# A fused decoder layer in fp32: latent attention's first queries in a stream of their own, stores on GpSimd's queue, first bias rows earlier

## The chip, the cores and the metric

The kernel runs on one core of a Trainium2 chip. The metric is device time in microseconds (us) of one execution; lower is better. Engines are named as in the profile: PE (TensorE matrix multiplies), DVE (VectorE), ACT (ScalarE), POOL (GpSimd), SP (SyncE, which here only issues DMAs).

## The reference

One decoder layer over 1024 tokens of width 1024, all in float32. Three mixers share one input projection and one output projection; then comes a mixture of experts. Only the mixers matter for this change:

```python
def hybrid_mixer(x, w_in, w_out, sink, bias_a, bias_b, q_norm_g, kv_norm_g, w_uq, w_ukv, cos, sin):
    h = x @ w_in
    h_a, h_b, h_c = jnp.split(h, [A_COLS, A_COLS + B_COLS], axis=-1)
    o_a = swa_sink_mixer(h_a, sink, bias_a)
    o_b = dilated_mixer(h_b, bias_b)
    o_c = mla_mixer(h_c, q_norm_g, kv_norm_g, w_uq, w_ukv, cos, sin)
    return jnp.concatenate([o_a, o_b, o_c], axis=-1) @ w_out

def mla_mixer(...):
    q = (rms_norm(c_q, q_norm_g) @ w_uq).reshape(Bsz, T, C_HEADS, C_NOPE + C_ROPE)
    kv = (rms_norm(c_kv, kv_norm_g) @ w_ukv).reshape(Bsz, T, C_HEADS, C_NOPE + C_V)
...
        s = jnp.where(key_pos[None, :] <= q_pos[:, None], s, NEG_INF)
        p = jax.nn.softmax(s, axis=-1)
        return jnp.einsum('bhqk,bkhd->bqhd', p.astype(v.dtype), v)
```

Mixer A is banded attention with a window of 128 (4 heads), mixer B three groups of dilated banded attention (4 heads each), each with a learned bias by distance. Mixer C is latent attention: 8 heads, dense and causal, with keys of 64 + 32 columns and values of 64. After them come a layer norm, the choice of an expert group and of 2 out of 32 experts a token, the experts, and a second layer norm.

## The kernel before

Every large product is made of three matmuls on split operands (`mm3`, lines 388 to 390: high x high, low x high, high x low), so each operand is first cut in a high part (ACT, line 376 or 380) and a low part (DVE, line 378 or 382).

The program is written as tasks. A task issues matmuls on PE and then steps on other engines; it names the tasks that it needs and the buffers that it takes and frees. `Order.run` (line 301) takes lists of tasks (streams) and writes all engines' instructions out in one order: at each turn it takes, among the heads of all streams, the task that can start first by its own cost table, and between those that tie, the stream that stands first in `STREAMS`. So the order on each engine is fixed when the program is built, and each engine works through its instructions in that order: one that waits holds up all that stand behind it on its engine.

The stages in order of time, from the profiled execution: input projections (to about 430 us, with mixers B and A between them from 137 us on), latent attention (about 445 to 615 us), output projection and choice of experts (to 724 us), 32 experts (to 1030 us), the last layer norm.

Of the projections of latent attention (`mla_units`), keys, values and queries are stored to DRAM in split form (`d_k`, `d_v`, `d_qr`, `d_qn`; function `out`, line 1299, 56 stores of 256 KB on SP's queue), and loaded again per head (`kqs`, lines 1431 to 1435) when latent attention begins; `vC` holds the values (line 1443).

The bias of mixer B's first group (g = 2 in `row_tasks`, line 476) is made so: POOL clears a small tile `ohr` and loads a one-hot table into it (lines 483, 484) and casts it to `oh` (486); PE multiplies it with the bias table (`psb`, 491); ACT copies out the rows (494); POOL stores them (`d_row`, 496), moves them skewed in DRAM (`d_shear`, 498) and loads the table `tb` (508). DVE needs `tb` to turn the first scores `S_B` into `P_B` (744).

In latent attention (`dense`, line 1459) scores `SC` go to PE, the masked maximum to DVE (1488), exponentials to ACT (1494), transposes `ptC` to PE (1517), the product with values `oC` to PE (834, 835). `fs_A` and `fs_C` (864) spread the normalizing factors `fb_A`, `fb_C`, which ACT writes (859), over the rows; `fs_A` belongs to the end of mixer A. Between these runs `part_tasks`: the part of the output projection that needs only mixers A and B's outputs. It loads them as `ofa` (POOL, 1608, four loads in all), cuts them to `oha`, multiplies (`ya`, 16 tasks of 12 matmuls), and adds the result to `xr` (DVE, 1636), which POOL stores (`d_zp`, 1637). The rest of the projection is `y`, from `oh`.

Of the kernel before, what the change touches and what calls it, by code (L numbers as in the profile page):

```python
# [51 lines left out]
WPOOL = ((0, 0), (0, 1))  # L52
OPOOL = ()
MMB = 6
STREAMS = 'VTGRLQNPlE'
LAT = 0.415
TIE = 0.06
EARLY = 2
# [284 lines left out]
class K:  # L343
# [534 lines left out]
    def phase_attention(self):  # L878
# [58 lines left out]
        def mixed(a, b):  # L937

            return [t for i, x in enumerate(a) for t in b[i * len(b) // len(a):(i + 1) * len(b) // len(a)] + [x]]

        for ui, u in enumerate(units):
            nm = u[2] if u[0] == "cols" else u[1]
            if u[0] == "mla":
                M[nm] = self.mla_units(ui, nm, lat)
                if nm == "q":
                    Pt += M["r"][:1] + mixed(M["k"] + M["v"], early["v"]) + mixed(M["r"][1:], early["q"][:4])
                    Pt += rowt[2][0] + mixed(M["q"], early["q"][4:])
            elif u[0] == "v":
                def begin(nm=nm):
                    vt[nm] = self.vp.tile([P, 8, 2, 4, HD], F32R, name="v" + nm, tag="v")  # L950
                    if nm == "B0":
                        vt["A"] = self.vp.tile([P, 8, 1, 4, HD], F32R, name="vA", tag="va")

                def dests(nm=nm):
                    d = [(0, 2, vt[nm])]
                    return d + [(256, 1, vt["A"]), (384, 0, kr)] if nm == "B0" else d

                if nm != "B0":
                    tk = self.v_tasks(ui, u, None, None, [])
                    last["v" + nm] = self.dilated_v(int(nm[1]), u[2], tk[1::2])  # L960
                    if nm == "B1":
                        early["v"] = list(tk)
                    else:
                        Pt += tk
                else:
                    tk = self.v_tasks(ui, u, begin, dests, ["v", "va"])
                    tk[0].deps = [last["vB2"]]
                    Pt += tk
                    last["v" + nm] = tk[-1]
                    krt = self.key_rope_tasks(kr, tk[-1])  # L970
                    Pt += krt
            elif nm[0] == "c":
                j = int(nm[1])

                pt_, lt_ = self.latent_unit(ui, u, "kv" if j == 2 else "q", 128 if j == 2 else 256, lat, j != 1,
                                            (2,) if j == 2 else (0, 1) if j == 1 else None)
                if ui == 0:
                    first2 = pt_
                elif ui == 1:
                    both = []  # L980
                    for i in range(4):
                        for t in (first2[2 * i:2 * i + 2] + pt_[2 * i:2 * i + 2]):
                            t.deps.append(there[2 * i + 1])
                            both.append(t)
                    Pt += both
                else:
                    Pt += pt_
                L += lt_
            else:
                cells[nm] = []  # L990
                bq[nm] = [Buf("qk"), Buf("qk")]
                tk = self.qk_tasks(ui, u, cells[nm], bq[nm])
                if ui == 7:
                    early["q"] = list(tk)
                    tk[0].deps = [lat["t", j] for j in range(3)]
                else:
                    Pt += tk
                last[nm] = tk[-1]
            for g in rows:
                if rows[g] == ui:  # L1000
                    Pt += rowt[g][1]
                if rows[g] == ui + 1 and g != 2:
                    Pt += rowt[g][0]
# [274 lines left out]
    def mla_units(self, u, which, lat):  # L1278
# [17 lines left out]

        def out(dst, t):
            for i in range(2):
                nc.sync.dma_start(dst(i), t[i].bitcast(F32))

        kw = dict(deps=deps, alloc=["mm", "ph"], free=["mm", "ph"])
        steps = [("A", 0.48), ("D", 0.6), ("A", 0.48), ("D", 0.6), ("T", 2.5)]
# [134 lines left out]
    def mla_tasks(self, deps, tr):  # L1437

        nc = self.nc
        self.sm = {}  # L1440

        def vload(b):
            nc.sync.dma_start(self.v[:, b].rearrange("p (g h) i d -> p g (h i d)", g=2).bitcast(F32), self.d_v[b])

        ld = [Task(lambda n=n: self.kq_load(n), 0, [[("T", 4.0)]], deps=deps + ([tr] if n % NSET else []),
                   alloc=["kq%d" % (n % NSET)] + (["v"] if n == 0 else [])) for n in range(8)]
        vt = [Task(lambda b=b: vload(b), 0, [[("T", 4.0)]], deps=[tr]) for b in range(8)]
        Q, TT, V = [], [], []
        for n in range(8):
            if n % 2 == 0:  # L1450
                cell = {}
            for qp in range(4):
                q, t, v = self.dense(n, qp, ld, vt, tr, cell)
                Q += q
                TT += t
                V += v
        return ld[:1] + vt[:2] + ld[1:2] + vt[2:4] + ld[2:3] + vt[4:] + ld[3:], Q, TT, V

    def dense(self, n, qp, ld, vt, tr, cell):

# [2 lines left out]
        nm = "C%d_%d" % (n, qp)  # L1463
        p, hd = divmod(n, 2)
        hf = qp // 2
        Q, TT, V = [], [], []
        Ps = {}

# [30 lines left out]
        for b in (2 * qp, 2 * qp + 1):  # L1499
# [3 lines left out]
            post = [("D", 0.08 + 0.00104 * w) for w in ws] + [("A", 0.2 + 0.00083 * w) for w in ws]  # L1503
            Q.append(Task(lambda b=b: qfn(b), sum(3 * max(0.109, w * 0.000417) for w in ws), post,
                          deps=[ld[n], tr], alloc=["mm"] * len(ws) + [pb[b]], free_at={i + 1: ["mm"] for i in range(len(ws))}))
        if qp == 3:
            Q[-1].free_pe = ["kq%d" % (n % NSET)]
        nk = 2 * qp + 2
        for j0 in range(0, nk, 2):
# [17 lines left out]
            first, last = qp % 2 == 0 and j0 == 0, qp % 2 == 1 and j0 == nk - 2  # L1527
            if first:
                cell["ob"] = Buf("o")
            if last and hd == 0 and hf == 0:  # L1530
                cell["otb"] = Buf("ot")

            def vfn(j0=j0, slots=slots, st=st, first=first, last=last):
                if first:
                    cell["o"] = self.buf("o", [P, 512], F32, name="o" + nm)
                o = cell["o"]
                for j in (j0, j0 + 1):
                    mine = [s for s, (jj, i) in enumerate(slots) if jj == j]
                    s0, w = mine[0] * P, len(mine) * P
                    c0 = (qp % 2) * 256 + slots[mine[0]][1] * P  # L1540
                    vh = self.v[:, j, n]
                    self.pv(o[:, c0:c0 + w], (vh.rearrange("p i d -> p (i d)"), vh[:, 0]),
                            [st[i][:, s0:s0 + w] for i in range(2)], first and j == j0)
                yield
                if last:
                    if hd == 0 and hf == 0:
                        cell["ot"] = self.buf("ot", [P, T], F32, name="o" + nm)
                    yield from self.unfold(cell["ot"][hd * HD:(hd + 1) * HD, hf * 512:(hf + 1) * 512], o, hd)

            V.append(Task(vfn, 0.43, [("A", 0.48), ("D", 0.6)] if last else [], deps=[tt, vt[j0 + 1]],  # L1550
                          alloc=([cell["ob"]] if first else []) + ([cell["otb"]] if last and hd == 0 and hf == 0 else []),
                          free=[cell["ob"]] if last else [], free_pe=["ph"]))
        if qp % 2 and hd:
            def factor():
                l = sm["l"][:, 4 * hf:4 * hf + 4, 2 * p:2 * p + 2, :]
                r = sm["rl"][:, 4 * hf:4 * hf + 4, 2 * p:2 * p + 2]
                nc.vector.tensor_tensor(r, l[:, :, :, 0], l[:, :, :, 1], ALU.add)
                nc.vector.reciprocal(r, r)

            def use(ps):  # L1560
                ot = cell["ot"][:, hf * 512:(hf + 1) * 512]
                nc.vector.tensor_tensor(ot, ot, ps, ALU.mult)
                nc.sync.dma_start(self.d_o[4 + p, :, hf * 512:(hf + 1) * 512], ot)

            ft = Task(factor, 0, [[("D", 0.2)]], deps=[Q[-1]])
            sp = self.spread_tasks(nm, lambda: sm["rl"][:, :, 2 * p:2 * p + 2], hf, use, [ft, V[-1]], [cell["otb"]] * hf)
            sp[0].deps = [ft]
            sp[1].deps = sp[1].deps + [V[-1]]
            V += [ft] + sp
# [440 lines left out]
    def phase_mixers(self):  # L2010

        self.wos = {}
        Pt, Q, TT, V, L, krt, vl = self.phase_attention()
        tr = Task(self.mla_open, 0, deps=[Pt[-1]] + L)
        ld, Q2, T2, V2 = self.mla_tasks(krt, tr)
        part, pl, wl, w1, xl, ya = self.part_tasks([tr, V[-1]])
        for n, b in YAQ:
            Q2[n].deps = Q2[n].deps + [ya[b, 1]]
        Y, R, G, E = self.out_tasks(Q2 + wl + w1, V2, w1, ya[7, 1])
        m = dict(E=E, V=[V + V2], R=R, T=[TT + T2], Q=[Q + Q2], L=[L], N=[vl], P=[Pt + [tr] + part + Y], l=[ld, pl, wl, xl], G=G)  # L2020
        self.ord.run([s for k in STREAMS for s in m[k]])


# [468 lines left out]
```

## Time and profile before

| | before |
|---|---|
| median of 3 runs | 1091.59 us (1088.22 to 1093.24) |
| profiled execution, its own time | 1088.41 us |
| its span, first to last instruction | 1086.7 us |
| mean granted clock of TensorE | 0.967 |
| PE busy | 1014.6 us, 93% of the span |
| DVE, ACT, POOL busy | 759.6, 689.7, 212.5 us |
| moved by DMA | 231.06 MB, mean 213 GB/s |

The sum of a change is made against the profiled execution, 1088.41 us; what lies around its span is 1.7 us. That execution is 3.2 us below the median of the three runs. A granted clock of 1 is 2.4 GHz, of 0.5 it is 1.2 GHz. Busy time of PE counts work at either clock.

### The profile page before, as it was taken

How to read it: one execution, taken by the hardware profiler on the slowest of the kernel's cores; microseconds unless marked ns; L12 is line 12 of the kernel's file. 1: busy time of each engine (PE TensorE's matmuls, PEld its weight loads, DVE VectorE, ACT ScalarE, POOL GpSimd, SP SyncE). 2: the span in 40 equal slices, each digit the busy share in tenths (PEclk: the TensorE clock that was granted, in tenths of full speed). 3: DMA queues.
4: the chain of work that ended last, by engine and by line, in shares of the span. 5: the costliest groups of instructions: out<-in, count | busy, mean ns of one | idle time of the engine just before them, and what ended most of it. 6: DMA issues, size and time to landing. Idle time of an engine off the chain costs nothing. (4 is left out here: it accounts for less than half of the span.)

```text
span 1086.7 us, 16593 instructions
## 1 busy us (share of the span) xinstructions
PE 1014.6 (93%) x5703; PEld 841.5 (77%) x5703; DVE 759.6 (70%) x1610; ACT 689.7 (63%) x1453; POOL 212.5 (20%) x235
## 2 busy tenths in 40 slices
PE   8998989999999998899999998969999999999971
PEld 7897878988798887788889777757777777777730
DVE  5465556345444657889687558789899999999747
ACT  5343456255443556889666435449999888898764
POOL 1011001501100203003100134422334222221123
PEclk9998989999999999999999999989999999999986
DMA  7177713422503234383662584649999999999283
GB/s 281 41 294 268 280 42 118 153 85 84 115 26 93 74 92 127 107 288 84 196 179 68 161 313 156 271 163 332 379 371 387 391 382 379 388 384 366 113 321 153
DMA packets 68631, 231.06 MB, mean 213 GB/s; under 512 B 13012, under 2 KB 18580, under 8 KB 54976
## 3 DMA queue, kind: packets, MB, share of 16 engines
q1 hardware_dynamic: 50064, 180.64, 47.1%
q0 software_dynamic: 17616, 46.18, 12.1%
q10 hardware_dynamic: 864, 3.15, 0.7%
q8 instruction: 46, 0.75, 0.3%
q14 instruction: 41, 0.34, 0.1%
HBM read 191.82 MB, written 58.02 MB: 230 GB/s over the span
## 5 line engine op out<-in xcount | busy, mean ns | idle before, releaser
L2192 DVE TENSOR_TENSOR el<-er,eh 128x1024 fp32r<-128x1024 f32 x188 | 226.1, 1221 | 22.4 <-ACT eh L2190 22.4
L2190 ACT CAST eh<-er 128x1024 fp32r<-128x1024 f32 x188 | 193.7, 1057 | 5.0 <-PE gu L390 3.1
L389 PE MATMUL gu<-el,xh 128*128 128x512 f32 x256 | 104.9, 410 | 0.0
L388 PE MATMUL gu<-eh,xh 128*128 128x512 f32 x256 | 103.8, 406 | 0.0
L390 PE MATMUL gu<-eh,xl 128*128 128x512 f32 x256 | 101.2, 395 | 1.0 <-DVE xl L378 1.0
L2025 POOL DMA_INDIRECT xg<-d_x,tok x32 | 43.7, 1367 | 159.4 <-PE gx L2208 138.0
L1494 ACT ACTIVATE PC<-PC,mnC 128x512 f32<-128x512 f32 (+3 forms) x96 | 58.6, 616 | 20.0 <-DVE mnC L1488 19.8
L389 PEld LDWEIGHTS gu<-el,xh 128*128 128x128 f32 x256 | 48.2, 188 | 21.7 <-DVE el L2192 12.9
L388 PE MATMUL psv_B<-wh,xH 128*128 128x256 f32 (+1 forms) x192 | 60.4, 315 | 1.7 <-ACT wh L376 1.7
L389 PE MATMUL psv_B<-wl,xH 128*128 128x256 f32 (+1 forms) x192 | 59.5, 310 | 0.2 <-DVE wl L378 0.2
L748 ACT ACTIVATE P_B<-P_B,negm_B 128x128 f32<-128x128 f32 (+1 forms) x96 | 42.4, 443 | 26.4 <-DVE negm_B L744 26.4
L390 PE MATMUL psv_B<-wh,xL 128*128 128x256 f32 (+1 forms) x192 | 59.1, 308 | 0.0
L2030 POOL DMA_INDIRECT d_y<-y,idx x32 | 40.3, 1259 | 90.5 <-ACT y L2247 84.1
L390 PEld LDWEIGHTS gu<-eh,xl 128*128 128x128 f32 x256 | 48.1, 188 | 10.7 <-DVE xl L378 1.4
L388 PEld LDWEIGHTS gu<-eh,xh 128*128 128x128 f32 x256 | 48.1, 188 | 10.1
L388 PE MATMUL y<-eh,hh 128*128 128x512 f32 x128 | 52.8, 412 | 0.7 <-ACT hh L376 0.7
L378 DVE TENSOR_TENSOR plC<-ptC,phC 128x512 fp32r<-128x512 f32 (+1 forms) x80 | 46.7, 630 | 7.0 <-ACT phC L376 6.6
L389 PE MATMUL y<-el,hh 128*128 128x512 f32 x128 | 50.6, 395 | 0.0
L390 PE MATMUL y<-eh,hl 128*128 128x512 f32 x128 | 50.4, 393 | 0.0
L376 ACT CAST phC<-ptC 128x512 fp32r<-128x512 f32 (+1 forms) x80 | 38.7, 548 | 8.5 <-PE ptC L1517 8.2
L378 DVE TENSOR_TENSOR xl<-gx,xh 128x512 fp32r<-128x512 f32 x64 | 43.5, 684 | 0.0
L2247 ACT COPY y<-y 128x512 f32<-128x512 f32 x64 | 37.6, 588 | 8.3 <-PE y L390 4.4
(452 smaller groups left out, 2903.6 us busy)
## 6 DMA issues: line engine op xcount, KB each, us to landing
er<-in_w_gu SPq DMA_DIRECT2D x63, 1024.0 KB, 16.5
er<-in_w_dn SPq DMA_DIRECT2D x32, 1024.0 KB, 15.2
wr<-in_w_qk SPq DMA_DIRECT2D x36, 256.0 KB, 3.9
fy<-d_y SPq DMA_DIRECT2D x7, 1024.0 KB, 11.8
d_vb<-vs_B POOLq DMA_DIRECT2D x16, 256.0 KB, 2.7
kqs<-d_k SPq DMA_DIRECT2D x16, 256.0 KB, 4.8
kqs<-d_qn SPq DMA_DIRECT2D x16, 256.0 KB, 4.8
vC<-d_v SPq DMA_DIRECT2D x8, 512.0 KB, 6.3
```

The lines of the kernel that those rows point to most:

```text
L376: nc.scalar.copy(h, src)
L378: (low or nc.vector).tensor_tensor(l, src, h.bitcast(F32), ALU.subtract)
L388: nc.tensor.matmul(out, st[0], mv[0], start=start, stop=False, **kw)
L389: nc.tensor.matmul(out, st[0], mv[1], start=False, stop=False, **kw)
L390: nc.tensor.matmul(out, st[1], mv[0], start=False, stop=stop, **kw)
L748: nc.scalar.activation(p[:, i, :w], p[:, i, :w], AF.Exp, bias=negm()[:, b, hh:hh + 1], scale=-1.0, accum_out=l()[:, b, hh:hh + 1])
L1494: nc.scalar.activation(pt[:, c:c + w], pt[:, c:c + w], AF.Exp, bias=mn[:, 1:2], scale=-1.0, accum_out=sm["l"][:, b, n, i:i + 1])
L2025: self.nc.gpsimd.indirect_dma_start(out=xg, out_offset=None, in_=self.d_x1, in_offset=bass.IndirectOffsetOnAxis(ap=tok.bitcast(U32), axis= ...
L2030: return self.nc.gpsimd.indirect_dma_start(out=self.d_y, out_offset=bass.IndirectOffsetOnAxis(ap=idx.bitcast(U32), axis=0), in_=y, in_offs ...
L2190: nc.scalar.copy(hi[:, s], t[:, s])
L2192: nc.vector.tensor_tensor(lo[:, s], t[:, s], hi[:, s].bitcast(F32), ALU.subtract)
L2247: nc.scalar.copy(y[e][:, s], ps)
```

## The change

Three things are changed.

1. The first two score tasks of latent attention (head 0) leave the queries' stream and form a stream `q` of their own, one place later in priority. For the first two heads the query pairs are taken in the order 2, 3, 0, 1, and not 0, 1, 2, 3; the buffers of the keys and of the output are taken and freed to suit. Six of the eight loads of values are put ahead of the second head's keys.
2. `out` in `mla_units` issues its 56 stores from POOL and no longer from SP.
3. The matmuls of the first bias rows (`rowt[2][1]`) stand after the sixth task of the latent queries, and no longer at the end of their unit.

```diff
-STREAMS = 'VTGRLQNPlE'
+STREAMS = 'VTGRLQqNPlE'
...
-                    Pt += rowt[2][0] + mixed(M["q"], early["q"][4:])
+                    mq = mixed(M["q"], early["q"][4:])
+                    Pt += rowt[2][0] + mq[:6] + rowt[2][1] + mq[6:]
...
-                if rows[g] == ui:
+                if rows[g] == ui and g != 2:
                     Pt += rowt[g][1]
...
         def out(dst, t):
             for i in range(2):
-                nc.sync.dma_start(dst(i), t[i].bitcast(F32))
+                nc.gpsimd.dma_start(dst(i), t[i].bitcast(F32))
...
-            for qp in range(4):
+            for qp in ((2, 3, 0, 1) if n < 2 else range(4)):
...
-        return ld[:1] + vt[:2] + ld[1:2] + vt[2:4] + ld[2:3] + vt[4:] + ld[3:], Q, TT, V
+        return ld[:1] + vt[:6] + ld[1:2] + vt[6:] + ld[2:], Q, TT, V
...
+        order = (1, 0) if p == 0 else (0, 1)
...
-        if qp == 3:
+        if qp % 2 and hf == order[1]:
             Q[-1].free_pe = ["kq%d" % (n % NSET)]
...
-        m = dict(E=E, V=[V + V2], R=R, T=[TT + T2], Q=[Q + Q2], L=[L], ...
+        m = dict(E=E, V=[V + V2], R=R, T=[TT + T2], Q=[Q + Q2[2:]], q=[Q2[:2]], L=[L], ...
```

Each engine issues the same instructions as before, in another order; only the 56 stores change queue. From the first `y` matmul on, PE's order is the same as before. Three places show what moved (a row is a line of the program, an operation, and output and inputs with their sizes; a line after the edits has one or two added).

**POOL, the first bias rows.** The difference, with `qr` and `q` the rotary and plain latent queries on their way to DRAM:

```order
+L1300 DMA d_qr_77<-qr11h_1094 128x512
+L1300 DMA d_qr_77<-qr11l_1095 128x512
 L483 MEMSET ohr2_1103 33x384
 L484 DMA ohr2_1103<-in_c_onehot 33x383
 L486 CAST oh2_1106<-ohr2_1103 33x384
-L496 DMA d_row_82<-rows2_1260 4x383
-L498 DMA d_shear_83<-d_row_82 128x1532
-L508 DMA tb2_1335<-d_shear_83 128x4x256
+L1300 DMA d_qn_76<-q0_0h_1108 128x512
+L1300 DMA d_qn_76<-q0_0l_1109 128x512
+L1300 DMA d_qn_76<-q0_1h_1124 128x512
+L1300 DMA d_qn_76<-q0_1l_1125 128x512
```

Before, clearing and loading `ohr` followed the loads of `vB`; now eight stores of rotary queries stand ahead of them, of which the last two are shown. Behind the cast of `oh` stand eight stores of plain queries (four shown), then `d_row`. On PE the two `psb` matmuls stand 36 matmuls of 512 columns sooner than before: right behind the fourth tile of plain queries, and no longer behind the eighth.

**PE, the end of mixer A.** `S_A` are the last scores of mixer A's second pair but for one block, `fs_A` and `pt_A` its factors and transposes. Before:

```order
L390 MATMUL S_A_4_1_4507<-h_kA,l_qA_4126 128x256
L864 MATMUL fs_A_0_4600<-ident,fb_A_0_4573 128x128 x4
L777 MATMUL pt_A_0_0_4611<-ident,P_A_0_0_4504 128x128 x2
L777 MATMUL pt_A_0_1_4616<-ident,P_A_0_1_4525 128x128 x2
L864 MATMUL fs_A_1_4623<-ident,fb_A_1_4609 128x128 x4
```

Now, up to the second `fs_A`:

```order
L390 MATMUL S_A_4_1_4507<-h_kA,l_qA_4126 128x256
L388 MATMUL SC_2_4_0_4603<-kqs_4311 128x512
L389 MATMUL SC_2_4_0_4603<-kqs_4311 128x512
L390 MATMUL SC_2_4_0_4603<-kqs_4311 128x512
L388 MATMUL SC_2_4_512_4607<-kqs_4311 128x128
L389 MATMUL SC_2_4_512_4607<-kqs_4311 128x128
L390 MATMUL SC_2_4_512_4607<-kqs_4311 128x128
L864 MATMUL fs_A_0_4617<-ident,fb_A_0_4573 128x128 x4
L777 MATMUL pt_A_0_0_4627<-ident,P_A_0_0_4504 128x128 x2
L864 MATMUL fs_A_1_4636<-ident,fb_A_1_4625 128x128 x4
```

Six score matmuls of latent attention's query block 4 come between, and six more of block 5 follow behind the next transposes. The first `ya` has about as much PE work ahead of it as before.

**POOL and PE, the end of latent attention.** POOL before, where `d_zp` stores a finished tile of `ya` and `ofa` is the load for the last four `ya`:

```order
L1637 DMA d_zp<-xr_1_6762 128x512
L1637 DMA d_zp<-xr_0_6764 128x512
L1608 DMA ofa_6919<-d_o 128x4x256
L1637 DMA d_zp<-xr_1_6766 128x512
L1637 DMA d_zp<-xr_0_6921 128x512
L1637 DMA d_zp<-xr_0_6964 128x512
```

POOL now:

```order
L1639 DMA d_zp<-xr_1_6579 128x512
L1610 DMA ofa_6826<-d_o 128x4x256
L1639 DMA d_zp<-xr_0_6581 128x512
L1639 DMA d_zp<-xr_1_6828 128x512
L1639 DMA d_zp<-xr_0_6830 128x512
L1610 DMA ofa_6965<-d_o 128x4x256
L1639 DMA d_zp<-xr_1_6832 128x512
```

And PE now, where the last load's `ya` begin:

```order
L390 MATMUL ya_1_6950<-woh_1_5309,oha_6869 128x512
L388 MATMUL ya_1_6950<-woh_1_5311,oha_6869 128x512
L389 MATMUL ya_1_6950<-wol_1_5312,oha_6869 128x512
L390 MATMUL ya_1_6950<-woh_1_5311,oha_6869 128x512
L388 MATMUL ya_0_6983<-woh_0_5297,oha_6975 128x512
L389 MATMUL ya_0_6983<-wol_0_5298,oha_6975 128x512
```

The last `ofa` stands behind the eleventh of sixteen `d_zp`, before and now. Before, PE had fifteen transposes, the twelfth `ya`, the last sixteen `oC` and `fs_C` between the eleventh `ya` and the first that needs this load; now only the twelfth `ya` lies between. Eight `ya` follow the last `oC` on PE, where it was four, and two of the eight come ahead of the last `fs_C`, which before followed that `oC` at once. On ACT and DVE the order of all of latent attention is new as well.

## Rows read from the trace of the kernel before

**Rows 1.** Page, part 1: busy time of each engine, share of the span, instructions.

```profile
PE 1014.6 (93%) x5703; PEld 841.5 (77%) x5703; DVE 759.6 (70%) x1610; ACT 689.7 (63%) x1453; POOL 212.5 (20%) x235
```

**Rows 2.** Timelines of ScalarE and PE, 87 to 89 us: start, us, row, idle before and releaser.

```profile
87.94 1.15 ACT L376 CAST wh<-wr 128x512 fp32r<-128x512 f32 x2
...
88.62 0.50 PE L388 MATMUL ps_qB<-xH,wh 128*128 128x512 f32 x1 [2.20 <-ACT wh L376]
```

**Rows 3.** Answer on one tensor: the values' stores, shortest, median and longest in ns.

```profile
L671 POOL DMA_DIRECT2D d_vb<-vs_B x16: 539/540/565, 55.8 to 209.1; - x16
```

**Rows 4.** Timeline of GpSimd, the first bias rows and the next one-hot load.

```profile
93.60 0.44 POOL L483 MEMSET ohr<- 33x384 f32 x1
94.33 0.58 POOL L484 DMA_DIRECT2D ohr<-in_c_onehot  x1 [0.29 <-POOL ohr L483]
112.70 0.49 POOL L486 CAST oh<-ohr 33x384 fp32r<-33x384 f32 x1 [17.79 <-DVE qr11l L378]
125.17 0.53 POOL L496 DMA_DIRECT2D d_row<-rows  x1 [11.97 <-ACT rows L494]
...
135.20 0.80 POOL L508 DMA_DIRECT2D tb<-d_shear  x1 [4.67 <-DMA d_shear<-d_row]
...
136.72 0.55 POOL L484 DMA_DIRECT2D ohr<-in_c_onehot  x1 [0.29 <-POOL ohr L483]
140.72 0.50 POOL L486 CAST oh<-ohr 33x384 fp32r<-33x384 f32 x1 [3.44 <-DMA ohr<-in_c_onehot]
```

**Rows 5.** Timeline of VectorE, the two rows that end GpSimd's and PE's waits.

```profile
111.88 0.69 DVE L378 TENSOR_TENSOR qr11l<-t,qr11h 128x512 fp32r<-128x512 f32 x1 [0.73 <-ACT qr11h L376]
...
140.56 0.29 DVE L744 CUSTOM_DVE_ANT_0 P_B<-S_B,tb 128x128 f32<-128x128 f32 x1 [6.19 <-DMA tb<-d_shear]
```

**Rows 6.** Timeline of PE around the bias rows and the first scores.

```profile
111.81 0.40 PE L388 MATMUL mpq<-ch,wh 128*128 128x512 f32 x1
...
120.24 0.33 PE L491 MATMUL psb<-oh,relbh 33*4 33x384 f32 x1
...
141.26 0.59 PE L388 MATMUL S_B<-h_kB,h_qB 64*128 64x128 f32 x2 [3.08 <-DVE negm_B L744]
```

**Rows 7.** Waits of GpSimd, whole span, for the one-hot table's load.

```profile
POOL oh L486 <- DMA ohr<-in_c_onehot: 12.6, 3, 5.8
```

**Rows 8.** By stretch: length, busy PE, PEld, DVE, ACT, POOL (x rows), clock, DMA share, GB/s.

```profile
141.20:147.20 6.00, 5.94 (x24) 5.23 (x25) 3.92 (x22) 4.82 (x21) 0.01 (x1) 0.50 0.00 0
429.70:460.60 30.90, 25.44 (x185) 21.22 (x185) 25.02 (x81) 24.25 (x76) 0.55 (x1) 0.94 0.42 121
460.60:518.80 58.20, 56.35 (x415) 51.47 (x414) 51.11 (x140) 53.11 (x144) 11.41 (x10) 1.00 0.63 187
518.80:612.50 93.70, 93.24 (x602) 83.52 (x601) 67.88 (x165) 56.56 (x147) 8.72 (x15) 1.00 0.48 142
614.60:618.30 3.70, 3.70 (x12) 3.05 (x13) 1.50 (x3) 0.45 (x1) 0.00 (x0) 0.54 0.25 91
```

**Rows 9.** Timeline of PE, the wait at the start of latent attention.

```profile
435.02 0.66 PE L864 MATMUL fs_A<-ident,fb_A 128*128 128x128 f32 x4 [2.94 <-ACT fb_A L859]
```

**Rows 10.** Timelines of PE, VectorE, GpSimd and ScalarE, 606 to 630 us.

```profile
614.59 0.93 PE L864 MATMUL fs_C<-ident,fb_C 128*128 128x128 f32 x4 [1.83 <-ACT fb_C L859]
...
629.13 0.50 PE L388 MATMUL y<-woh,oh 128*128 128x512 f32 x1 [1.18 <-ACT oh L1719]
...
606.63 0.69 DVE L1636 SCALAR_TENSOR_TENSOR xr<-xr,ya 128x512 f32<-128x512 f32 x1 [2.11 <-PE ya L390]
...
607.61 0.54 POOL L1637 DMA_DIRECT2D d_zp<-xr  x1 [2.25 <-DVE xr L1636]
608.15 0.76 POOL L1608 DMA_DIRECT2D ofa<-d_o  x1
...
613.40 0.62 ACT L376 CAST oha<-ofa 128x512 fp32r<-128x512 f32 x1
```

**Rows 11.** Answer on one tensor: landing of the load of mixer A's outputs.

```profile
DMA to landing us min/median/max: 7.4/7.4/7.4
```

More of the change, by code (lines that the diff above doesn't have):

```diff
@@ L1529, in dense @@
                 cell["ob"] = Buf("o")
-            if last and hd == 0 and hf == 0:
+            if last and hd == 0 and hf == order[0]:
                 cell["otb"] = Buf("ot")
@@ L1545, in vfn @@
                 if last:
-                    if hd == 0 and hf == 0:
+                    if hd == 0 and hf == order[0]:
                         cell["ot"] = self.buf("ot", [P, T], F32, name="o" + nm)
@@ L1550, in dense @@
             V.append(Task(vfn, 0.43, [("A", 0.48), ("D", 0.6)] if last else [], deps=[tt, vt[j0 + 1]],
-                          alloc=([cell["ob"]] if first else []) + ([cell["otb"]] if last and hd == 0 and hf == 0 else []),
+                          alloc=([cell["ob"]] if first else []) + ([cell["otb"]] if last and hd == 0 and hf == order[0] else []),
                           free=[cell["ob"]] if last else [], free_pe=["ph"]))
@@ L1565, in dense @@
             ft = Task(factor, 0, [[("D", 0.2)]], deps=[Q[-1]])
-            sp = self.spread_tasks(nm, lambda: sm["rl"][:, :, 2 * p:2 * p + 2], hf, use, [ft, V[-1]], [cell["otb"]] * hf)
+            sp = self.spread_tasks(nm, lambda: sm["rl"][:, :, 2 * p:2 * p + 2], hf, use, [ft, V[-1]], [cell["otb"]] * (hf == order[1]))
             sp[0].deps = [ft]
@@ L2019, in phase_mixers @@
         Y, R, G, E = self.out_tasks(Q2 + wl + w1, V2, w1, ya[7, 1])
-        m = dict(E=E, V=[V + V2], R=R, T=[TT + T2], Q=[Q + Q2], L=[L], N=[vl], P=[Pt + [tr] + part + Y], l=[ld, pl, wl, xl], G=G)
+        m = dict(E=E, V=[V + V2], R=R, T=[TT + T2], Q=[Q + Q2[2:]], q=[Q2[:2]], L=[L], N=[vl], P=[Pt + [tr] + part + Y], l=[ld, pl, wl, xl], G=G)
         self.ord.run([s for k in STREAMS for s in m[k]])
```

## Prediction

> **What bounds the kernel now.** I read the busy times first: PE works 93% of the span and no other engine over 70% [rows 1]. PE takes its instructions in a fixed order, so a change in order is worth what PE idles, and what TensorE's clock loses after PE has idled; a busy stretch can give nothing. The stretches [rows 8] show where idle time is left in latent attention: 5.5 us of 30.9 at its start, 1.9 us of the next 58.2, 0.5 us of the last 93.7. The start also has a granted clock of 0.94, which loses 0.06 x 30.9 = 1.9 us. All that a better order could win there is 5.5 + 1.9 + 0.5 + 1.9 = 9.8 us. Then I read the timelines where the change puts hands on: PE's wait ahead of the first scores of mixer B, 3.08 us [rows 6], which ends when VectorE has `tb` [rows 5]; PE's wait for `fb_A`, 2.94 us [rows 9]; and those at the end of latent attention, 1.83 and 1.18 us [rows 10]. After the first of these the clock stood at 0.50 for 6.0 us, after the third at 0.54 for 3.7 us [rows 8]: lost 3.0 and 1.7 us. So a wait of PE costs itself and up to 3 us more.
>
> **Stores on GpSimd's queue.** SP loses 56 issues. Would its weight loads, which stood behind them, free PE? PE's one long wait among the latent units, 2.20 us, ends with a cast on ScalarE that starts with no idle time ahead of it [rows 2]: ScalarE was busy, not short of data, and its order there is unchanged. So 0; were a late weight load behind it after all, the bound is a gain of 2.2 + 3.0 = 5.2 us. On GpSimd a store of this size takes 0.54 us to issue [rows 3]. The 40 stores of keys, values and `vs_B` between 55.8 and 93.6 us take 40 x 0.54 = 21.6 us of 37.8, so GpSimd keeps up. The stored tensors are next read when latent attention loads its heads, some 300 us later; that covers any later landing.
>
> Those 16 samples also weigh a rule. The Trainium skill (SBUF — State Buffer, the section on two separate sides, and the one on the bandwidth-pool intuition) says that a DMA issued from GpSimd waits while VectorE holds the port that both share, and gives 620 ns alone and 3100 ns beside a VectorE copy. By it the 40 stores would take an estimated 124 us and GpSimd would run some 86 us late. The longest of the 16 is 565 ns beside a working VectorE; the trace does not agree, and this stands below as a rival of small weight.
>
> **First bias rows.** `psb` moves 36 matmuls forward: from 120.24 to 111.81 us [rows 6], 8.4 us. But the one-hot table that it needs is late. Before, its load was issued at 94.33 us [rows 4], long ahead. Now GpSimd, in order, first has the store of `qr11l` in its queue, which waits for VectorE to end at 111.88 + 0.69 = 112.57 [rows 5]. Then come 0.54 for that store, 0.44 to clear, 0.29 + 0.55 to issue the load, the landing, and 0.50 for the cast [rows 4]. Landing is the unknown: 3.44 us in the next case [rows 4], 5.8 at most over three [rows 7]. `oh` is there at 118.3 to 120.7, about when it was used before, and PE, which stands at `psb` from 111.8, waits 6.5 to 8.9 us. I take the middle, 7.7. What the clock loses afterwards is bounded by 1.7 and 3.0; I take 3.0, from the wait nearest in length. Queued behind that load are sixteen stores of plain queries, `d_row`, `d_shear` and `tb`. Eight stores come before `d_row`: 120.7 + 4.3 = 125.0, as early as before (125.17), and from there to VectorE's use of `tb` took 15.4 us [rows 4, 5]; with the other eight stores' 4.3 that ends by 144.7. PE reaches the scores 6.5 to 8.9 us later than the 138 it stood there, so by 144.7 to 147. The old wait of 3.08 and its 3.0 of clock are gone. Sum: 7.7 + 3.0 - 6.1 = **+4.6 us** (bounds 6.5 + 1.7 - 6.1 = +2.1 and 8.9 + 3.0 - 6.1 = +5.8). The wait for rows has moved from `tb` to `oh` and grown.
>
> **Latent attention's first scores.** Six score matmuls now stand ahead of the first `fs_A`, and more behind it, in PE's wait of 2.94 us [rows 9]; if that wait goes, the half clock of this stretch (1.9) goes too: **-4.8 us**. What is late next is ScalarE: busy 24.25 of these 30.9 us [rows 8], it gets the exponentials of those scores earlier, among the last ones of mixer A and ahead of the second pair's factors. So the gain may be nothing, or the wait may come back there (+2.9); at best all idle time and clock of the three stretches goes (-9.8). I take the two named items, half of that. The values' loads now ahead of the second head's keys cost nothing: head 0 alone is a stage of many microseconds, and four loads at about half a microsecond of issue each stand in front.
>
> **End of latent attention.** Two `ya` (24 matmuls, 5.6 us at 8.43 / 36 = 0.234 each) now fill the wait of 1.83 us for `fb_C`, and the 1.18 us ahead of `y` have four more `ya` in front: gone are 1.83 + 1.7 + 1.18 = 4.7 us. But the last `ofa` is now due one `ya` after the store that stands ahead of it on GpSimd. From the end of that `ya`: 0.98 to the store's issue, 0.54 for it, 0.76 for the load's issue, landing, 0.62 for the cast. Before, it had landed by 613.40, 4.5 us after its issue or sooner [rows 10]; the other bounds are 3.44 for the one-hot load and 7.4 us from issue to landing for the one `ofa` that was seen [rows 11]. PE has one `ya` in hand, 2.8 us. Wait: 0.98 + 0.54 + 0.76 + 4.5 + 0.62 - 2.8 = 4.6 us, and the clock's 1.7 of this place: 6.3 - 4.7 = **+1.6 us** (3.5 + 1.7 - 4.7 = +0.5 to 6.7 + 3.0 - 4.7 = +5.0). From `y` on nothing moves; all later work starts as much later or sooner.
>
> **Sum.** 0 + 4.6 - 4.8 + 1.6 = +1.4 us on the profiled 1088.41, so 1089.8 for that execution. It lies 3.2 us below the median of the three runs; on the median of 1091.59 the forecast is **1093.0 us**. About 0.5%, 5.5 us, is what a measurement of this kernel can tell from no change: no visible change.
>
> **Rivals.**
> - *ScalarE sets the pace* (slower, 0.25). At the end of mixer A and in the first two heads ScalarE and VectorE are busy 24 to 25 of 30.9 us and 51 to 53 of 58.2 [rows 8], so scores put early only push mixer A's exponentials and `fb_A` back. It decides from the point at which the new exponentials ahead of the second `fb_A` take longer than the new score matmuls on PE. Then the start gives 0 to +2.9: +6.2 to +9.1, about 1099. Against it: PE's wait falls where VectorE and ScalarE have gaps too.
> - *GpSimd's new waits do not bite* (faster, 0.12): `qr11l` and the loads come early enough that `psb` and the last `ya` wait under 1 us each. Then -5.1 - 4.8 - 3.7 = -13.6, 1078. This is what the change says it does. Against it stands GpSimd's order.
> - *The new order keeps PE full* (faster, 0.15): all 9.8 us are won and GpSimd's waits are at their short ends: +2.1 - 9.8 + 0.5 = -7.2, 1084.4.
> - *GpSimd falls behind its stores* (slower, 0.03): each issue stretches several times over, as it did in none of the 16; the queue's delay goes one to one into `psb`, and to fall behind at all takes 37.8 / 40 = 0.95 us an issue. At 1.3 us it would be 40 x 1.3 - 37.8 = 14 us late: about 1107 or above. The Trainium skill's page on SBUF is the ground for it.
>
> **How the numbers follow.** The forecast has 0.45; its own bounds, with the start of latent attention held, are 1091.59 + 2.1 - 4.8 + 0.5 = 1089.4 and 1091.59 + 5.8 - 4.8 + 5.0 = 1097.6. For 8 in 10 the range takes in the slower rival to 1101 and the second faster one, down to 1083; left out are the first faster rival, the last one and the far edges. Chances: faster 0.12 + 0.15 = 0.27, same 0.45, slower 0.25 + 0.03 = 0.28.
>
> **What would show it.** In the new profile: a wait of PE at `psb` of 6.5 to 8.9 us that ends on GpSimd's cast of `oh`, a half clock behind it, and no wait for `tb`. No wait of 2.9 us at the first `fs_A`, and a clock of about 1 from 430 to 461 us of the old time. At the end no wait at the last `fs_C`, but one of 3.5 to 6.7 us at the `ya` that needs the last `ofa`. From the first `y` on, the same length as before. The prediction is wrong if PE does not wait at `psb`, if the second `fs_A` waits as long as the first did, or if GpSimd's issues last more than 0.6 us.

## The result and the profile after

| | before | after |
|---|---|---|
| median of 6 runs each, one chip | 1089.76 us (1087.74 to 1093.24) | 1098.61 us (1095.14 to 1101.45) |
| ratio, 95% interval | | 1.0066 [1.0037, 1.0095] |
| span of the profiled execution | 1086.7 us | 1097.4 us |
| mean granted clock | 0.967 | 0.967 |

By the ratio the change costs 7.2 us [4.0, 10.4]; the medians of six lie 8.9 us apart. The forecast was +1.4 us, "no visible change"; the measured time lies within its range, but beyond the 0.5%, near the rival that was priced at about 1099. One run further on, of `after_prep_ofa`, took 2067.27 us for a cause that is not known and is left out of its ratio.

Page, part 1, of the kernel after, against [rows 1]:

```profile
PE 1014.6 (92%) x5703; PEld 839.7 (77%) x5703; DVE 758.8 (69%) x1610; ACT 690.0 (63%) x1453; POOL 240.9 (22%) x291
```

PE does the same work in the same busy time; the loss is idle time. POOL has 56 instructions and 28.4 us more. Waits of PE after (releaser, us in total, times, longest), those that the prediction spoke of or that changed:

```profile
PE psb L491 <- POOL oh L486: 5.6, 1, 5.6
...
PE ya L388 <- ACT oha L376: 5.1, 1, 5.1
PE ps_c L388 <- ACT xH L366: 3.5, 1, 3.5
PE ps_qB L388 <- ACT wh L376: 3.4, 1, 3.4
...
PE ptC L1519 <- ACT PC L1496: 1.6, 1, 1.6
...
PE SC L388 <- DVE negm_A L744: 1.3, 1, 1.3
PE y L388 <- ACT oh L1721: 1.2, 1, 1.2
...
PE fs_A L864 <- ACT fb_A L859: 0.4, 1, 0.4
```

The wait ahead of the first `S_B` [rows 6] is gone, that for `fb_A` has fallen from 2.94 [rows 9] to 0.4, that at the last `fs_C` (1.83) is gone, as a row below shows, and that ahead of `y` [rows 10] stands as it was. New are `psb`, `ya`, `SC` for `negm_A` and `ptC` for `PC`. (A wait at `psv_B` for `wh` is 1.7 us before, 2.7 here and 0.8 in the second profile of after: chance.) GpSimd's timeline after shows what `psb` and `ya` waited for:

```profile
114.26 0.54 POOL L1300 DMA_DIRECT2D d_qr<-qr11h  x1 [2.21 <-ACT qr11h L376]
114.99 0.54 POOL L1300 DMA_DIRECT2D d_qr<-qr11l  x1 [0.19 <-issue]
115.52 0.44 POOL L483 MEMSET ohr<- 33x384 f32 x1
116.25 0.56 POOL L484 DMA_DIRECT2D ohr<-in_c_onehot  x1 [0.29 <-POOL ohr L483]
119.19 0.50 POOL L486 CAST oh<-ohr 33x384 fp32r<-33x384 f32 x1 [2.39 <-DMA ohr<-in_c_onehot]
...
123.97 0.52 POOL L496 DMA_DIRECT2D d_row<-rows  x1
...
135.65 0.78 POOL L508 DMA_DIRECT2D tb<-d_shear  x1 [3.09 <-DMA d_shear<-d_row]
...
617.39 0.54 POOL L1639 DMA_DIRECT2D d_zp<-xr  x1 [2.68 <-DVE xr L1638]
617.92 0.76 POOL L1610 DMA_DIRECT2D ofa<-d_o  x1
```

The table's clearing stands behind the store of `qr11l`, and the cast 2.39 us behind its issue. `d_row` went out at 123.97, 1.2 us sooner than before, and `tb` at 135.65, 0.4 us later [rows 4]; counted from this trace's late start, 2.8 us by 49 us (table below), that is 4.0 and 2.4 us sooner. PE has no wait for `tb` left, but one of 5.6 us at `psb`. PE's timeline at the new waits, at the end of mixer A, and at three of the `fs_C`:

```profile
119.74 0.48 PE L491 MATMUL psb<-oh,relbh 33*4 33x384 f32 x1 [5.64 <-POOL oh L486]
...
436.18 0.50 PE L388 MATMUL SC<-kqs 96*128 96x512 f32 x1 [1.31 <-DVE negm_A L744]
440.19 1.11 PE L864 MATMUL fs_A<-ident,fb_A 128*128 128x128 f32 x4 [0.42 <-ACT fb_A L859]
...
486.37 0.66 PE L864 MATMUL fs_C<-ident,fb_C 128*128 128x128 f32 x4 [0.67 <-ACT fb_C L859]
...
515.31 0.63 PE L864 MATMUL fs_C<-ident,fb_C 128*128 128x128 f32 x4 [0.91 <-DVE plC L378]
...
603.25 1.75 PE L1519 MATMUL ptC<-ident,PC 128*128 128x128 f32 x14 [1.60 <-ACT PC L1496]
...
612.99 0.60 PE L864 MATMUL fs_C<-ident,fb_C 128*128 128x128 f32 x4
...
624.24 0.79 PE L388 MATMUL ya<-woh,oha 128*128 128x512 f32 x1 [5.07 <-ACT oha L376]
```

And the stretches (columns as in [rows 8]): around `psb`, behind `SC`, behind the last `fs_C`, around `ya`, then latent attention in three parts.

```profile
116.00:123.00 7.00, 3.26 (x8) 2.13 (x9) 2.39 (x4) 1.54 (x3) 4.34 (x9) 0.53 0.65 234
436.30:444.00 7.70, 7.13 (x27) 5.57 (x28) 7.28 (x31) 7.56 (x28) 0.56 (x1) 0.57 1.04 227
612.90:616.60 3.70, 3.70 (x20) 3.04 (x18) 1.48 (x3) 0.00 (x0) 0.54 (x1) 1.00 0.43 156
620.90:628.20 7.30, 3.96 (x9) 3.09 (x10) 1.29 (x2) 1.14 (x2) 0.00 (x0) 0.55 0.60 206
432.80:463.70 30.90, 27.73 (x191) 23.13 (x188) 26.91 (x85) 26.54 (x82) 0.56 (x1) 0.89 0.71 209
463.70:521.40 57.70, 54.30 (x406) 49.83 (x405) 48.74 (x133) 51.48 (x138) 12.22 (x11) 1.00 0.64 175
521.40:607.60 86.20, 84.30 (x557) 75.08 (x556) 63.52 (x162) 55.54 (x147) 5.11 (x9) 1.00 0.38 110
```

After the waits at `psb`, `SC` (1.3 us only) and `ya`, PE worked at half clock for 3 to 7 us; behind the last `fs_C` the clock stands at 1. In latent attention PE is idle for 3.2 + 3.4 + 1.9 = 8.5 us where it was 5.5 + 1.9 + 0.5 = 7.9 [rows 8]: the start has less, the two later parts more; 0.67, 0.91 and 1.60 us of it are the waits at 486, 515 and 603 us. And the start's clock fell from 0.94 to 0.89.

To place the loss I matched PE's instructions of two traces by name and compared their starts. Each figure is what a kernel lost in that segment (us) against the first profile of before:

| profile | to 49 us | to the first `S_A` (407) | to the first `y` (629) | to the last expert (1021) |
|---|---|---|---|---|
| before, second profile | +2.1 | -2.7 | +0.3 | +0.8 |
| after | +2.8 | 0.0 | +6.9 | +0.4 |
| after, second profile | +1.9 | -1.1 | +7.1 | +0.4 |

The first segment is the same code in all of them and differs by chance: its wait `ps_c` was 3.5 us in one profile and 1.8 in another. The second spreads by 2.7 between two executions of before. The loss that stands out is that between `S_A` and `y`: the end of mixer A and latent attention. What the second segment costs has to come from the runs.

### The profile page after: what moved, and what is told of

Read it like the earlier page. It is cut to its first block, busy times and chain, and to the rows that moved or that the text cites. A ratio compares the mean times of both kernels' runs of the same rounds, so it can differ in the third digit from the quotient of the medians.

```text
span 1097.4 us, 16609 instructions
## 1 busy us (share of the span) xinstructions
PE 1014.6 (92%) x5703; PEld 839.7 (77%) x5703; DVE 758.8 (69%) x1610; ACT 690.0 (63%) x1453; POOL 240.9 (22%) x291
## 4 chain that ended last, share of the span: by engine, by line
PE 72%; DVE 9%; issue 7%; DMA 6%; ACT 5%; POOL 1%; SPq 0%; DVEq 0%; POOLq 0%; ACTq 0%
PE gu L389 6%; PE gu L390 5%; PE gu L388 5%; PE y L388 4%; PE y L390 4%; PE y L389 4%; PE psv_B L388 2%; PE psv_B L389 2%; PE psv_B L390 2%; PE ps_qB L390 2%; PE ps_qB L388 2%; PE gx L2210 2%; PE ps_qB L389 2%; PE ps_kB L388 2%; PE ps_kB L390 2%
## 5 line engine op out<-in xcount | busy, mean ns | idle before, releaser
L388 PE MATMUL ps_qB<-xH,wh 128*128 128x512 f32 x96 | 40.0, 417 | 3.4 <-ACT wh L376 3.4
```

Of the source, the lines that this page charges most:

```text
L388: nc.tensor.matmul(out, st[0], mv[0], start=start, stop=False, **kw)
```

## The experiments

The parts are numbered as in the change. Each ratio is to before on the same chip, and the three groups ran on three chips; 12 runs of a kernel where no other number is given.

**1. The parts by themselves.** Before: 1088.52 us, median of 35 runs. Streams and order in latent attention alone (`p1_streams`) is the change with two edits undone:

```diff
-                    Pt += rowt[2][0] + mq[:6] + rowt[2][1] + mq[6:]
+                    Pt += rowt[2][0] + mixed(M["q"], early["q"][4:])
...
-                nc.gpsimd.dma_start(dst(i), t[i].bitcast(F32))
+                nc.sync.dma_start(dst(i), t[i].bitcast(F32))
```

> Part 1 alone (stream q, query pairs 2,3,0,1 for heads 0 and 1, six value loads first); stores on SP and bias rows as before. Theory (the loss sits in latent attention's order): its offset to before is 0 up to the last S_A and about +7 us at the first y (+3 by the last oC, +4 at the wait for the last ofa), so +6 to +7 us, ratio about 1.006. Rival (GpSimd's stores carry the loss, in the waits for oh and ofa): 0 to +1 us, ratio 1.000 to 1.001.

1094.67 us, 1.0056 [1.0035, 1.0078]; its trace loses 6.7 us between `S_A` and `y`, with a wait for `oha` of 4.9 us. So this part costs 6.1 us and not the -3.2 of the prediction.

The stores alone (`p2_stores`) is before with that one line of `out` on GpSimd.

> Part 2 alone: the 56 stores on GpSimd's queue, PE's order as before. Theory: no PE wait is removed; d_row now stands behind the query stores, so the wait for tb may grow by up to 1 us: 0 to +1 us. Rival (the stores carry the loss): +6 to +7 us, and a wait at psb. Second rival (the late start, +2.8 us by 14 us, belongs to the stores): its profile shows the same late start.

1091.13 us, 1.001 [0.9986, 1.0033]: no cost that this interval can tell from none.

The rows alone (`p3_rows`) is before with `rowt[2][1]` moved as in the change, stores on SP.

> Part 3 alone: bias rows 36 matmuls sooner, stores on SP. Theory: without the stores ahead of it the one-hot load is early; oh waits only for its buffer, which VectorE frees at 112.6 us, so PE waits 1.4 us at psb instead of 5.6, and the 3.1 us wait for tb with its 3.0 us of half clock goes: -3 to -5 us, ratio about 0.996. Rival (rows sooner give nothing, since PE's wait only changes place): 0.

1083.95 us, 0.9951 [0.9928, 0.9974], faster than before and than the change. Waits of PE hold none at `S_B`, and `psb` waits shortly. Timelines of GpSimd and PE there:

```profile
94.33 0.44 POOL L483 MEMSET ohr<- 33x384 f32 x1
...
112.35 0.49 POOL L486 CAST oh<-ohr 33x384 fp32r<-33x384 f32 x1 [16.71 <-DVE qr11l L378]
115.10 0.53 POOL L496 DMA_DIRECT2D d_row<-rows  x1 [2.26 <-ACT rows L494]
...
112.90 0.33 PE L491 MATMUL psb<-oh,relbh 33*4 33x384 f32 x1 [1.28 <-POOL oh L486]
```

With nothing ahead of it on GpSimd the table is loaded long before, `d_row` goes out 10 us sooner than in [rows 4], and the clock stays at 1 behind the short wait.

Stores and rows together (`p23_stores_rows`):

> Parts 2 and 3, latent attention as before. Theory: the wait moves from tb (3.1 us and 3.0 of clock) to psb (5.6 and about 2.3): +1 to +2 us at most, ratio 1.000 to 1.002; the loss of the whole change is gone with part 1. Rival (stores carry it): +6 to +7 us.

1093.57 us, 1.0039 [1.0018, 1.006], somewhat above what was expected, with `psb` waiting 5.7 us. The rows that win 5 us alone lose 4 with the stores, a difference of 9.6 us (0.9951 against 1.0039). How much of it is their meeting on one queue, a repair below tells.

**2. Repairs.** Before: 1087.12 us, median of 29. If the two queue waits are the cost, taking `ofa` and the one-hot load out from behind GpSimd's stores must give it back. `p1_ofa_act` is `p1_streams` with one line changed:

```diff
-                nc.gpsimd.dma_start(r, self.d_o.rearrange("k p t -> p k t")[:, 0:4, b * P:(b + 2) * P])
+                nc.scalar.dma_start(r, self.d_o.rearrange("k p t -> p k t")[:, 0:4, b * P:(b + 2) * P])
```

> Part 1 with the four loads ofa issued from ScalarE's queue and not from GpSimd's; PE's order is that of part 1 alone, word for word. Theory (the last ofa waits on GpSimd behind the store of a ya that has just ended): PE's wait of 4.9 us at the ya that needs it and its 2 us of half clock go, -5 to -6 us against part 1, ratio to before 1.000 to 1.001. Rival (the new order of PE itself costs, the wait only shows where): the time stays at ratio 1.0056 and the wait turns up elsewhere.

1088.52 us, 1.0008 [0.999, 1.0027]: some 5 us of part 1's 6.1 were the late `ofa`. What is left is no gain. Its waits of PE at the places in question:

```profile
PE oC L834 <- ACT phC L376: 1.7, 1, 1.7
...
PE ya L390 <- DVE oha L378: 0.9, 1, 0.9
```

The wait of 1.7 us in the middle of latent attention (half clock from 499 to 502.5 us behind it) is no mark of the repair: the same row waits 1.0 us in the first profile of after and 1.7 in the second. The half clock at the start lasts as in after.

`p23_prep` clears and loads the table ahead of the stores, at the head of the latent queries:

```diff
-        def load():
+        def prep():
             cell["raw"] = self.pp.tile([33, NSH + 1], F32, name="ohr%d" % g, tag="fb")
...
-                    Pt += M["r"][:1] + mixed(M["k"] + M["v"], early["v"]) + mixed(M["r"][1:], early["q"][:4])
+                    Pt += rowt[2][0][:1] + M["r"][:1] + mixed(M["k"] + M["v"], early["v"]) + mixed(M["r"][1:], early["q"][:4])
```

> Parts 2 and 3 with the clearing and the load of the first one-hot table put ahead of all the stores on GpSimd; the cast stays where it was, every other engine's order is unchanged. Theory (the wait at psb is the in-order queue's): oh is there at 113.7 us of before's time, PE waits 1.5 to 2 us at psb and not 5.7, the clock holds or loses 1 us: -4 to -6 us against parts 2 and 3, ratio to before 0.995 to 0.999. Rival (stores on GpSimd cost time of their own, wherever rows stand): it stays at 1.003 or above.

1087.57 us, 1.0001 [0.9986, 1.0017], above the range expected; `psb` waits 2.0 us. The repair gives back 4 us of the 9.6. GpSimd's timeline shows why `psb` still waits 0.7 us longer than in `p3_rows`:

```profile
113.67 0.54 POOL L1305 DMA_DIRECT2D d_qr<-qr11l  x1 [0.19 <-issue]
114.21 0.52 POOL L490 CAST oh<-ohr 33x384 fp32r<-33x384 f32 x1
```

The cast needs the buffer that VectorE frees with `qr11l`, and that tensor's store, now on the same queue, goes ahead of it.

Both repairs on the whole change (`after_prep_ofa`):

> The whole change with both repairs (one-hot load first, ofa from ScalarE's queue). Theory: both waits that the change brought go, -9 to -11 us against the change, ratio to before 0.996 to 0.999. Rival: a third cost remains, ratio 1.002 or above.

1088.98 us, 1.0007 [0.9988, 1.0027]: 6 us of the 7.2 come back, fewer than the 9 to 11 expected, and no gain over before is left.

`p1_noq` has part 1 with the two score tasks back in the queries' stream, to see whether the stream of their own is what costs:

```diff
-        m = dict(E=E, V=[V + V2], R=R, T=[TT + T2], Q=[Q + Q2[2:]], q=[Q2[:2]], L=[L], ...
+        m = dict(E=E, V=[V + V2], R=R, T=[TT + T2], Q=[Q + Q2], q=[], L=[L], ...
```

> Part 1 without the stream q: the first two score tasks stay in the queries' stream, the pairs keep the order 2,3,0,1 and the value loads stand first. The planner then puts the last ofa behind the ninth d_zp, and two ya ahead of the last fs_C. Theory: no wait for oha, none at the last fs_C: about -3 us at y against before; the old wait of 2.9 us at the first fs_A is back with its 1.9 of half clock, and the stretch up to the last oC is at 0 to +1: ratio 0.997 to 0.999. Rival (the pair order is what costs): +2 us or more at the first ya, ratio 1.002 to 1.006.

A miss: 1095.9 us (6 runs), 1.0081 [1.0051, 1.0111]. Its waits of PE show why it tells nothing of the stream:

```profile
PE SC L388 <- DMA kqs<-d_qr: 4.0, 1, 4.0
PE fs_A L864 <- ACT fb_A L859: 3.6, 2, 2.9
```

The old wait for `fb_A` is back, as expected, but the rest of the order came out anew: at 584 us scores of a later head wait for their queries' load. One part of such an order can't be taken out alone.

**3. Do the stores cost by themselves?** Before: 1088.02 us, median of 23. Both repairs left some 0.5% to `p3_rows`. `p3_kv_pool` is `p3_rows` with the stores of keys and values alone on GpSimd, which all stand ahead of the rows' steps:

```diff
-                nc.sync.dma_start(dst(i), t[i].bitcast(F32))
+                (nc.gpsimd if which in ("k", "v") else nc.sync).dma_start(dst(i), t[i].bitcast(F32))
```

> Part 3 with only the stores of latent keys and values on GpSimd's queue (32 of the 56); the queries' stores stay on SP, and no store stands between the one-hot load and its use. All other engines' orders are those of part 3. Theory (only the place in GpSimd's order costs): equal to part 3 alone, ratio 0.994 to 0.997. Rival (a store costs more when GpSimd issues it, wherever it stands): half or more of the 0.5% between part 3 alone and the repaired parts 2 and 3 is back, ratio 0.998 to 1.001.

1087.15 us, 0.9987 [0.997, 1.0003] where `p3_rows` had 0.9951 [0.9928, 0.9974]: about 0.4%, so the rival's range, with intervals that barely touch and from two chips. ScalarE's timeline in `p3_rows`, stores on SP, at the last value tile:

```profile
87.30 0.37 ACT L1315 CAST vt7h<-mv 128x256 fp32r<-128x256 f32 x1 [0.32 <-PE mv L390]
...
88.78 1.15 ACT L376 CAST wh<-wr 128x512 fp32r<-128x512 f32 x2
```

The same in `p3_kv_pool`, then PE's row that waits for that `wh`:

```profile
90.24 0.37 ACT L1315 CAST vt7h<-mv 128x256 fp32r<-128x256 f32 x1 [1.33 <-DMA d_vb<-vs_B]
...
91.72 1.15 ACT L376 CAST wh<-wr 128x512 fp32r<-128x512 f32 x2
...
92.40 0.50 PE L388 MATMUL ps_qB<-xH,wh 128*128 128x512 f32 x1 [3.21 <-ACT wh L376]
```

Value tiles `vt` and `vs_B` take turns in one ring of buffers (`tag="ph"`). On GpSimd's queue the store of `vs_B` now follows the stores of values in the queue. The answer on that one store in `p3_kv_pool`:

```profile
L671 POOL DMA_DIRECT2D d_vb<-vs_B x1: 539/539/539, 85.4 to 85.4; - x1
...
  ACT vt7h L1315: 1.3, 1
...
DMA to landing us min/median/max: 4.7/4.7/4.7
```

In `p3_rows` it was issued at 83.47 us and `vt7h` began at 87.30 without waiting for it, so it had landed within 3.8 us. The later landing holds up ScalarE's cast, ScalarE is the engine that PE waits for there [rows 2], and PE's wait grows from 2.2 to 3.2 us. Of seven profiles with stores on GpSimd, three have this wait at `vt7h` (1.3 to 1.5 us, the change's own among them), and these three alone have 3.2 to 3.4 us at `ps_qB`; the other four, and all seven with those stores on SP, have 2.2. It is a matter of a microsecond whether the buffer is late, so not each execution pays.

This is 1 us in some executions, and not 4 us on the mean. The half clock behind `ps_qB` lasted 7 us here and 3.5 in `p3_rows`, but that does not follow the wait: it lasted 7 us behind 2.2 us in the first profile of before (last section), and 3.5 behind 3.4 us in that of after. What else the stores cost stays open.

`p3_p1_ofa`, `p3_rows` with part 1 and its repair, stores on SP:

> Parts 1 and 3 with the loads ofa on ScalarE's queue, all stores on SP: the change without what the runs showed to cost. Theory (the parts add up): part 3 alone at 0.995 plus the repaired part 1 at 1.001: ratio 0.995 to 0.997, so not better than part 3 alone. Rival (part 1 gains once the waits are gone): 0.993 or below.

1084.79 us, 0.9967 [0.995, 0.9983]: not better than the rows alone.

Second profiles of both kernels gave two rows of the table above.

> The kernel before, unchanged: a second profile of it. Theory (the late start, +2.8 us by 50 us in the change's profile, is chance of the execution and no part of the change): its first products start anywhere from 9.4 to 11.5 us, and behind 50 us its waits are those of the first profile. Rival (the late start belongs to the change): they start at 9.4 us again, with a wait of 1.7 us.

> The change, unchanged: a second profile. Theory: waits at psb of 5 to 6 us and at the ya that needs the last ofa of 4.5 to 5.5 us, as in the first; its start is free to differ by up to 3 us from the first.

1089.65 us for before and 1097.18 for after. After waits again 5.9 us at `psb` and 4.4 at `ya`, but 2.2 at `ps_qB`.

## Why the prediction was right and wrong

**Stores on GpSimd: 0 forecast; 1.1 [-1.5, 3.6] us measured alone, some 4 beside `p3_rows`.** The step that failed: "GpSimd keeps up" is true, but I looked for the readers of the stored data, 300 us later, and not for who takes the store's buffer next, two tiles later. The row read for cover, ScalarE busy without idle time ahead of `wh` [rows 2], said that a delay of ScalarE there goes one to one into PE. Shown are 1 us at `ps_qB` in three profiles of seven, and 0.7 us at `psb` behind the repair; the rest of the 4 has no row that explains it. The rival of the Trainium skill (SBUF — State Buffer, the sections on two separate sides and on the bandwidth-pool intuition) did not come: of 56 stores beside a working VectorE the longest issue was 0.58 us. But "the trace does not agree" said too much. The Trainium skill gives its 3100 ns for a VectorE copy. From 53 to 132 us VectorE's rows in the profile of after are operations on two tensors (`TENSOR_TENSOR`, `SCALAR_TENSOR_TENSOR`) and a reciprocal, so no run here tests that figure.

**First bias rows: +4.6 forecast, +4.2 [2.0, 6.5] measured** for parts 2 and 3 together. Mechanism and place held: the wait at `psb` ends on the cast of `oh`, GpSimd's queue makes it late, the wait for `tb` is gone. Its size was 5.6 and 5.9 us and not 7.7, since the table landed 2.4 us after its issue, sooner than either of my bounds (3.44 and 5.8). The clock lost 1.6 and not 3.0. The credit of 6.1 was that of one execution: in the second profile of before the wait was 2.3 us with 1.7 of clock, 4.0 (PE's row, then the stretch behind it, 0.51 the clock):

```profile
141.35 0.39 PE L388 MATMUL S_B<-h_kB,h_qB 64*128 64x128 f32 x2 [2.29 <-DVE negm_B L744]
...
143.20:146.70 3.50, 3.41 (x11) 2.93 (x12) 1.70 (x4) 2.91 (x12) 0.00 (x0) 0.51 0.00 0
```

So the forecast's own terms give 5.6 + 1.6 - 6.1 = +1.1, or +3.2 with the smaller credit, and the stores' own cost lies in the same +4.2: the agreement is partly luck.

**Start of latent attention: -4.8 forecast, -0.8 by the stretches. This is the step that failed most.** The wait for `fb_A` went as forecast, but the six score matmuls put in front of it wait themselves, 1.3 us, for a score bank that VectorE's pass over mixer A (`negm_A`) has to free. Half clock followed that wait too and lasted longer: 0.11 x 30.9 = 3.4 us lost by the stretch, where it was 1.9. So 3.2 + 3.4 = 6.6 us are lost there where it was 5.5 + 1.9 = 7.4: PE's earlier start was spent at half speed.

**Middle of latent attention: nothing forecast, +2.9 measured** (1.5 + 1.4 of new idle time by the stretches). The new order was priced only at its two ends, without a reason for the middle; PE waits there at 486, 515 and 603 us. `p1_ofa_act`, the late `ofa` repaired, shows all the rest of part 1 at +0.9 us [-1.1, 2.9]: the start, the middle, and what the end still wins.

**End of latent attention: +1.6 forecast, +3.6 by the rows.** The wait of 4.6 us was measured at 5.1 and 4.4; `ofa` came 4.9 us after its issue ended against 4.5 taken. The clock cost 2.0 after it (PE worked 4 us at half speed, from 624.2 to 628.2), against 1.7 taken. Of the credit of 4.7, the wait of 1.83 at the last `fs_C` and the 1.7 of clock behind it came; the 1.18 ahead of `y` did not. With these the sum is 5.1 + 2.0 - 1.83 - 1.7 = +3.6. The repair, which takes out the late `ofa` alone, gave back 5.2.

**The rival near 1099.** It had its fact right, that the engines beside PE set the pace at the start, but the row of `SC` names VectorE and not ScalarE; `fb_A` was not pushed back (`fs_A` waits 0.4 us), and the start, priced at 0 to +2.9, came out at -0.8. That the time came out near its price is luck: the loss lies in the middle and at the end.

**From `y` on**, nothing moved: +0.4 us. That was right.

So the time missed the forecast by 5.8 us, and latent attention alone by more: 4.0 at its start, 2.9 in its middle, 2.0 at its end. It was +5.7 by these rows, and part 1 cost 6.1 by the runs. Parts 1 and 2 + 3, 6.1 and 4.2 us, add up to more than the whole's 7.2; the intervals allow that, and whether there is more to it stays open. A buffer of its own for the one-hot table, free of GpSimd's queue and of `qr11l` both, was not tried. The best version run is the rows alone.

## What to carry to other kernels

Before a DMA is moved to another engine's queue, read what stands behind it on that engine and who takes its source buffer next; the far reader of the data says nothing about either. A wait that an earlier instruction is to fill goes only if that instruction has its own buffers free: look up who frees them, and when. Two edits that each look harmless can meet on one queue: run them apart (0.9951 and 1.001) and together (1.0039).

## What the hardware showed

How long PE stayed at half clock after the same wait differed between two executions of before. Stretches behind the `ps_qB` wait of 2.20 us, first profile:

```profile
88.90:92.40 3.50, 2.93 (x8) 1.97 (x8) 1.61 (x3) 0.79 (x2) 1.66 (x3) 0.54 0.99 304
92.40:95.90 3.50, 3.50 (x10) 2.73 (x9) 0.75 (x1) 0.84 (x2) 2.22 (x4) 0.50 0.91 235
```

And in the second profile:

```profile
92.00:95.50 3.50, 3.43 (x8) 2.76 (x9) 1.36 (x3) 0.85 (x2) 2.76 (x4) 0.51 0.92 255
95.50:99.00 3.50, 3.50 (x16) 2.82 (x16) 0.69 (x1) 0.60 (x1) 1.12 (x3) 1.00 0.87 238
```

The same wait cost 3.5 us by the clock once and 1.7 the other time (half of the time at half speed). With a few such waits this alone spreads single executions by several us, which is why a segment of one trace could not price the bias rows and the runs had to. And a short wait can be followed by half clock or not: at `SC` one of 1.3 us was, at `psb` neither 1.3 us in `p3_rows` nor 2.0 us in `p23_prep` was. The stretch behind the latter:

```profile
114.80:118.30 3.50, 3.50 (x15) 2.62 (x16) 2.38 (x4) 1.30 (x3) 3.50 (x7) 1.00 0.91 305
```
